# Attention stage of a hybrid mLSTM and attention layer: elementwise work moved from POOL to VectorE, a gate folded into a scaled eviction, and softmax denominators applied to the head's result

## The chip, the cores and the metric

One core of a Trainium2 chip runs the whole layer in one launch. The metric is the device time of that core in microseconds: the median of three runs before the change is 1370.47 us (1370.43 to 1371.47). Names used below: PE is TensorE, DVE is VectorE, ACT is ScalarE, POOL is GpSimd, and SP is SyncE, which issues the DMAs.

## The reference

The layer works on 512 tokens of width 1024 in float32. It runs a feed-forward block, a mixing block and a second feed-forward block, each as a modulated residual. The mixing block is what the change touches; cut to the parts that matter:

```python
z = u @ w_mix + b_mix                       # q, k, v of both branches, their gates
h_m = mlstm_chunkwise(q_m, k_m, v_m, i_m, f_m)            # 4 heads, 256 wide
y_a = jax.nn.sigmoid(o_m) * rms_norm(h_m, mlstm_norm_g)
# forgetting attention, 16 heads of 64
q, k = rms_norm(q, q_g), rms_norm(k, k_g)
F = jnp.cumsum(jax.nn.log_sigmoid(f_pre), axis=1)
logits = einsum(q_blk, k) * 64 ** -0.5 + (F_blk[..., :, None] - F[..., None, :])
p = softmax(where(causal, logits, -inf))
y_b = einsum(p, v)
merged = jax.nn.sigmoid(g_a) * (y_a @ w_branch_a) + jax.nn.sigmoid(g_b) * (y_b @ w_branch_b)
x = x + g2 * (merged @ w_out)
```

## The kernel before

Every float32 matrix product is made of three passes on PE with operands split into a high and a low part (mm3, L106 to L110: high x high, low x high, high x low). A weight arrives as a tile `raw` (L76 to L80, a DMA that SP issues, three buffers); `split` (L82 to L92) lets ACT copy its high part to `wh` (L89) and DVE subtract that to make `wl` (L91), four buffers each.

The program is written for a tile framework with a scheduler. It puts the instructions of each engine in an order of its own choice and places the semaphores; each engine then runs its list strictly in that order. A tile of a tag with n buffers waits until the n-th tile before it is no longer read.

The attention stage is the loop over n in 18 of `run` (L1024 to L1042), about 547 to 856 us of the span. PSUM serves it with four banks `g` for projections and four banks `t` for all else. For each of the 16 heads it takes these steps, staggered so that head n's scores, head n-1's transposes and head n-2's result are in flight together:

- `fox_s(n)`, L779 to L807: a DMA spreads the head's row of cumulative gates over the partitions (A0, L784); POOL adds the causal mask to it (Am, L787, 128x512). PE makes the scores of four query blocks in four t banks (L795, L796), DVE evicts them with bias and running minimum (L798, L802), and ACT takes the exponentials into S (L806), whose row sums become `sm`, one 128x4 tile.
- `fox_p(n-1)`, L809 to L838: DVE takes the reciprocal of sm (L813) and scales the four blocks of S by it (L816); PE transposes S (L824); ACT and DVE evict the result as high part Ph (L822) and low part Pl (L823).
- `fox_o(n-2)`, L840 to L858: eight matmuls with the split values fvt (L854) give the high and the low half of the values' product in two halves of a bank; ACT copies the one (yt, L857), DVE adds the other and writes 64 rows of yb (L858).
- `fox_t`, L749 to L777: for each pair of heads PE transposes the token tiles tk (L767), and ACT and DVE make the split q and k (fq, fk, klz; L772 to L776).

Between these steps the loop pulls pieces of projections (`fill`) that keep PE busy: `fox_qkv(g)` (L700 to L747) for groups of four heads, `gate` (L882 to L895) and, from head 12 on, `y_a` (L861 to L879). In `fox_qkv` the four token tiles tk hold q and k of four heads; after their mean squares, DVE makes the factors rq (L125 to L135) and POOL scales the four tiles (L728). The values are evicted with bias by DVE (vg, L733), and for each of four token blocks ACT writes the high parts of two pairs of heads (fvt, L736, two 128x128) and POOL the low parts (L737). In `y_a` ACT takes a tanh (L869), POOL turns it into 0.5 + 0.5 tanh (L870), and DVE multiplies it with the gain and the transposed mLSTM output from PSUM (ya, L877).

Of the kernel before, what the change touches and what calls it, by code (L numbers as in the profile page):

```python
# [11 lines left out]
F32 = mybir.dt.float32  # L12
F32R = mybir.dt.float32r
I32 = mybir.dt.int32
AF = mybir.ActivationFunctionType
# [5 lines left out]
P = 128  # L21
T = 512
NT = 4
D = 1024
NK = 8
# [21 lines left out]
class Layer:  # L47
# [568 lines left out]
    def v_mlstm(self, half, ap, ip):  # L616
        nc, w = self.nc, self.A["w_mix"][0]
        bb = self.bias_bcast([(VM + half * 512, 512)], ip)
        vt = []
        for i in range(2):  # L620
            pair = [ap.tile([P, NT, 258], F32R, name=self.nm("vm"), tag="vm", bufs=6) for _ in range(2)]
            nc.scalar.activation(pair[0][:, :, 256:258], self.onz, AF.Copy)
            nc.scalar.activation(pair[1][:, :, 256:258], self.onz, AF.Copy, scale=0.0)
            vt.append(pair)
        def done(tb, ps):
            f = self.tmp(ip, "vf")
            nc.vector.tensor_tensor(f, ps, bb, op=ADD)
            for i in range(2):
                hi, lo = vt[i]
                s = slice(i * 256, (i + 1) * 256)  # L630
                nc.scalar.activation(hi[:, tb, 0:256], f[:, s], AF.Copy)
                nc.vector.tensor_tensor(lo[:, tb, 0:256], f[:, s], hi[:, tb, 0:256], op=SUB)
        def mk(ch):
            def make():
                wh, wl = self.w_mov(w, ch * 256, VM + half * 512)
                return wh, wl, 2 * ch, 2
            return make
        self.vt[2 * half:2 * half + 2] = vt
        yield from self.u_gemm_tokens([mk(c) for c in range(4)], 512, done)
# [60 lines left out]
    def fox_qkv(self, g, ip):  # L700

        nc, sp, w = self.nc, self.sp, self.A["w_mix"][0]
        o = g * 256
        bb = self.bias_bcast([(QF + o, 256), (KF + o, 256)], ip)
        tok = [ip.tile([P, 512], F32, name=self.nm("tk"), tag="tok", bufs=4) for _ in range(NT)]
        ss = sp.tile([P, NT, 8], F32, name=self.nm("fs"), tag="fs", bufs=2)
        def done(tb, ps):
            nc.vector.tensor_tensor(tok[tb], ps, bb, op=ADD)  # L708
            j = self.tmp(ip, "fj")
            nc.scalar.activation(j, tok[tb], AF.Square)  # L710
            nc.vector.tensor_reduce(ss[:, tb, :], j.rearrange("p (h d) -> p h d", h=8), AX.X, ADD)
        def mk(ch):
            def make():
                sh = [P, 2, 512]
                rows = w[ch * 256:(ch + 1) * 256]
                r = self.raw(sh, [(lambda t, i=i: t[:, :, i * 256:(i + 1) * 256],
                                   rows[:, c + o:c + o + 256].rearrange("(k p) n -> p k n", p=P))
                                  for i, c in enumerate((QF, KF))])
                wh, wl = self.split(r, sh)
                return wh, wl, 2 * ch, 2  # L720
            return make
        yield from self.u_gemm_tokens([mk(c) for c in range(4)], 512, done)
        v = sp.tile([P, NT * 8], F32, name=self.nm("fv"), tag="fv", bufs=2)
        nc.vector.tensor_scalar(v, ss.rearrange("p b h -> p (b h)"), 1.0 / 64, EPS, op0=MUL, op1=ADD)
        r = self.rsqrt(v, NT * 8)
        for tb in range(NT):
            t3 = tok[tb].rearrange("p (h d) -> p h d", h=8)
            nc.gpsimd.tensor_tensor(t3, t3, r[:, tb * 8:(tb + 1) * 8].unsqueeze(2).to_broadcast([P, 8, 64]), op=MUL)  # L728
        bv = self.bias_bcast([(VF + o, 256)], ip)
        vt = [ip.tile([P, NT, 2, P], F32R, name=self.nm("fvt"), tag="vm", bufs=6) for _ in range(2)]  # L730
        def donev(tb, ps):
            f = ip.tile([P, 256], F32, name=self.nm("vg"), tag="t2", bufs=3)
            nc.vector.tensor_tensor(f, ps[:, :256], bv[:, :256], op=ADD)  # L733
            for pr in range(2):
                f2 = f[:, pr * P:(pr + 1) * P].rearrange("p (h d) -> p h d", h=2)
                nc.scalar.activation(vt[pr][:, tb, :, 0:64], f2, AF.Copy)  # L736
                nc.gpsimd.tensor_tensor(vt[pr][:, tb, :, 64:P], f2, vt[pr][:, tb, :, 0:64], op=SUB)  # L737
        def mkv(ch):
            def make():
                sh = [P, 4, 256]  # L740
                r = self.raw(sh, [(lambda t: t, w[ch * 512:(ch + 1) * 512, VF + o:VF + o + 256]
                                   .rearrange("(k p) n -> p k n", p=P))])
                wh, wl = self.split(r, sh)
                return wh, wl, 4 * ch, 4
            return make
        self.fx[g] = (tok, vt)
        yield from self.u_gemm_tokens([mkv(c) for c in range(2)], 256, donev)  # L747
# [31 lines left out]
    def fox_s(self, h, ip):  # L779
# [4 lines left out]
        nc.sync.dma_start(A0, self.A_d[h:h + 1, :].to_broadcast([P, T]))  # L784
        Am = ip.tile([P, T], F32, name=self.nm("Am"), tag="bc", bufs=4)
        b4 = lambda t: t.rearrange("p (b t) -> p b t", b=NT)
        nc.gpsimd.tensor_tensor(b4(Am), b4(A0), self.maskF[:, None, :].to_broadcast([P, NT, P]), op=ADD)  # L787
        S = ip.tile([P, 1280], F32, name=self.nm("S"), tag="p6", bufs=5)
        mn = sp.tile([P, NT, 2], F32, name=self.nm("mn"), tag="mn", bufs=4)
        sm = sp.tile([P, NT], F32, name=self.nm("sm"), tag="sm", bufs=4)  # L790
        for qb in range(NT):
# [12 lines left out]
                m = mn[:, qb, 1:2]  # L804
            ws = slice(o, o + (qb + 1) * P)
            nc.scalar.activation(S[:, ws], S[:, ws], AF.Exp, scale=-1.0, bias=m, accum_out=sm[:, qb:qb + 1])  # L806
        self.S[h] = (S, sm)  # L807

    def fox_p(self, h, ip):  # L809

        nc = self.nc
        S, sm = self.S[h]
        nc.vector.reciprocal(sm, sm)  # L813
        for qb in range(NT):
            ws = slice(P_OFF[qb], P_OFF[qb] + (qb + 1) * P)
            nc.vector.tensor_scalar(S[:, ws], S[:, ws], sm[:, qb:qb + 1], None, op0=MUL)  # L816
        Ph = ip.tile([P, 1408], F32R, name=self.nm("Ph"), tag="p6", bufs=5)
        Pl = ip.tile([P, 1408], F32R, name=self.nm("Pl"), tag="p6", bufs=5)
        nc.scalar.activation(Ph[:, 512:640], self.ident, AF.Copy, scale=0.0)
        nc.scalar.activation(Pl[:, 512:640], self.ident, AF.Copy, scale=0.0)  # L820
        def evac(b, n, o):
            nc.scalar.activation(Ph[:, o:o + n], b[:, :n], AF.Copy)  # L822
            nc.vector.tensor_tensor(Pl[:, o:o + n], b[:, :n], Ph[:, o:o + n], op=SUB)  # L823
        tr = lambda b, c, qb, kb: nc.tensor.transpose(b[:, c:c + P], S[:, P_OFF[qb] + kb * P:P_OFF[qb] + (kb + 1) * P], self.ident)  # L824
        b = self.tbank()
        for qb in range(NT):
            tr(b, qb * P, qb, 0)
        evac(b, 512, 0)
        b = self.tbank()
        tr(b, 0, 3, 3)  # L830
        for qb in range(1, NT):
            tr(b, qb * P, qb, 1)
        evac(b, 512, 640)
        b = self.tbank()
        for qb in range(2, NT):
            tr(b, (qb - 2) * P, qb, 2)
        evac(b, 256, 1152)
        self.S[h] = (Ph, Pl)  # L838

    def fox_o(self, h, ip):  # L840
# [10 lines left out]
        for kb, o, q0 in blk:  # L851
            for Px in (Ph, Pl):
                n += 1
                nc.tensor.matmul(po[:, q0:], vt[pr][:, kb, i % 2, :], Px[:, o:o + T - q0], start=n == 1, stop=n == 8)  # L854
        tmp = self.tmp(ip, "yt")
        ot = slice(64 - hb, 128 - hb)
        nc.scalar.activation(tmp[rows, :], po[ot, :], AF.Copy)  # L857
        nc.vector.tensor_tensor(self.yb[2 * g + pr][rows, :], po[rows, :], tmp[rows, :], op=ADD)  # L858


    def y_a(self, m, ap, ip):  # L861
# [5 lines left out]
        self.gemm_stat(ps, w, 0, T, range(4, 8))  # L867
        th = self.tmp(ip, "th")
        nc.scalar.activation(th, ps, AF.Tanh, scale=0.5, bias=self.hom[:, m:m + 1])  # L869
        nc.gpsimd.tensor_scalar(th, th, 0.5, 0.5, op0=MUL, op1=ADD)  # L870
        ht = ip.tile([P, NT, P], F32, name=self.nm("ht"), tag="tok", bufs=4)
        nc.sync.dma_start(ht, self.h_d[:, m * P:(m + 1) * P].rearrange("(b p) n -> p b n", p=P))
        b = self.tbank()
        for tb in range(NT):
            nc.tensor.transpose(b[:, tb * P:(tb + 1) * P], ht[:, tb, :], self.ident)
        ya = ap.tile([P, T], F32, name=self.nm("ya"), tag="qk", bufs=16)
        nc.vector.scalar_tensor_tensor(ya, b, self.colA[:, R_MG + m:R_MG + m + 1], th, op0=MUL, op1=MUL)  # L877
        self.ya[m] = ya
        yield  # L879

# [41 lines left out]
    def run(self):  # L922
        nc, tc, A = self.nc, self.tc, self.A
        gain = lambda r: self.colA[:, r:r + NK]
        self.x_d = self.dp.tile([T, D], F32, name="x_d")
        self.h_d = self.dp.tile([T, D], F32, name="h_d")
        self.g_d = [self.dp.tile([P, T], F32, name=f"g_d{i}") for i in range(2 * NK)]

        self.ntmp, self.xn_tiles = 5, self.xn_start
# [60 lines left out]
        with tc.tile_pool(name="att", bufs=1) as ip:  # L990
# [9 lines left out]
            nc.gpsimd.memset(self.onz[:, :, 1:2], 0.0)  # L1000
            self.hom = ip.tile([P, NK], F32, name="hom")
            nc.vector.tensor_scalar(self.hom, self.colA[:, R_OM:R_OM + NK], 0.5, None, op0=MUL)
            self.hgg = yp.tile([P, 2 * NK], F32, name="hgg")
            nc.vector.tensor_scalar(self.hgg, self.colA[:, R_GG:R_GG + 2 * NK], 0.5, None, op0=MUL)
            self.klz = [None] * 2
# [112 lines left out]
```

## Time and profile before

| | us |
|---|---|
| median of three runs | 1370.47 (1370.43 to 1371.47) |
| the profiled execution | 1369.97 |
| its span | 1367.9 |
| PE busy | 1345.7 |
| DVE busy | 795.1 |
| ACT busy | 557.0 |
| POOL busy | 115.5 |

The granted clock of TensorE is 0.999 of full speed throughout. A row of a group of instructions gives line, engine, operation, output and inputs (buffer numbers left out), shapes and count; after the first bar the busy time and the mean of one in ns; after the second the idle time of the engine just before them and what ended it. A row of the timeline gives start and length in us. A row of the waits gives who waited for what: us in total, times, longest. In the table by slices the columns are the stretch, its length, and the busy time of PE, of PE's weight loads, of DVE, ACT and POOL with their instruction counts.

### The profile page before, as it was taken

What the parts mean: (1) busy time and instruction counts of PE and PEld (TensorE: products, weight loads), DVE (VectorE), ACT (ScalarE), POOL (GpSimd) and SP (SyncE); (2) the same over time, 40 slices, a digit from 0 to 9 for tenths busy, and PEclk for the clock granted to TensorE, in tenths of its full rate; (3) what the DMA queues carried; (4) which work ended last, traced back from release to release, by engine and by line L of the source; (5) the groups of instructions that cost most, each with busy time, mean ns of one, the idle gap of its engine ahead of it and who ended that gap; (6) DMA issues with size and microseconds to landing.
All of it is one profiled execution on the core that took longest, in us unless ns stands there. A gap on an engine that the chain in (4) does not pass through costs nothing.

```text
span 1367.9 us, 17550 instructions
## 1 busy us (share of the span) xinstructions
PE 1345.7 (98%) x6586; PEld 1126.2 (82%) x6586; DVE 795.1 (58%) x1427; ACT 557.0 (41%) x953; POOL 115.5 (8%) x143
## 2 busy tenths in 40 slices
PE   7999999999999999999999999999999999999998
PEld 6788887877888888888888888888798888888886
DVE  6865666656467777785776775456473333332232
ACT  4542333323237655466655665332263223222120
POOL 2000000000011100321121311012010000000000
PEclk9999999999999999999999999999999999999999
DMA  9676556666534434434252542464323333333330
GB/s 289 189 216 194 182 182 191 216 214 192 184 79 110 124 94 129 144 90 137 57 155 62 162 108 70 131 192 145 94 78 108 94 105 95 92 100 101 100 123 31
DMA packets 216457, 183.37 MB, mean 134 GB/s; under 512 B 10866, under 2 KB 182546, under 8 KB 216372
## 3 DMA queue, kind: packets, MB, share of 16 engines
q1 hardware_dynamic: 215892, 182.17, 44.5%
q8 instruction: 52, 0.85, 0.3%
q14 instruction: 33, 0.27, 0.1%
q0 software_dynamic: 416, 0.06, 0.0%
q10 hardware_dynamic: 64, 0.02, 0.0%
HBM read 172.18 MB, written 10.03 MB: 133 GB/s over the span
## 4 chain that ended last, share of the span: by engine, by line
PE 90%; DVE 6%; ACT 3%; issue 1%; DMA 1%; SPq 0%; DVEq 0%; ACTq 0%
PE g L110 23%; PE g L108 23%; PE g L109 23%; PE t L108 4%; PE t L110 4%; PE t L109 4%; PE g L510 2%; PE t L854 2%; PE t L824 1%; DVE wl L91 1%; PE t L795 1%; PE t L796 1%; PE t L510 1%; DVE fq L774 0%; ACT uh L475 0%
## 5 line engine op out<-in xcount | busy, mean ns | idle before, releaser
L91 DVE TENSOR_TENSOR wl<-raw,wh 128x1024 fp32r<-128x1024 f32 x214 | 274.5, 1284 | 280.1 <-ACT wh L89 262.5
L89 ACT ACTIVATE wh<-raw 128x1024 fp32r<-128x1024 f32 x214 | 225.8, 1060 | 496.8 <-PE g L109 153.1
L108 PE MATMUL g<-uh,wh 128*128 128x512 f32 (+2 forms) x984 | 370.5, 377 | 0.5 <-ACT wh L89 0.5
L110 PE MATMUL g<-uh,wl 128*128 128x512 f32 (+2 forms) x984 | 369.7, 376 | 1.2 <-DVE wl L91 1.2
L109 PE MATMUL g<-ul,wh 128*128 128x512 f32 (+2 forms) x984 | 369.7, 376 | 0.0
L110 PEld LDWEIGHTS g<-uh,wl 128*128 128x128 f32 (+1 forms) x984 | 184.6, 188 | 35.9 <-DVE wl L91 2.0
L108 PEld LDWEIGHTS g<-uh,wh 128*128 128x128 f32 (+1 forms) x984 | 184.7, 188 | 34.4 <-ACT wh L89 1.2
L109 PEld LDWEIGHTS g<-ul,wh 128*128 128x128 f32 (+1 forms) x984 | 184.8, 188 | 33.2
L108 PE MATMUL g<-wh,uh 128*128 128x512 f32 (+1 forms) x320 | 111.9, 350 | 0.0
L110 PE MATMUL g<-wh,ul 128*128 128x512 f32 (+1 forms) x320 | 111.1, 347 | 0.0
L109 PE MATMUL g<-wl,uh 128*128 128x512 f32 (+1 forms) x320 | 111.0, 347 | 0.0
L325 DVE TENSOR_TENSOR sl<-g,sl 128x512 f32<-128x512 f32 (+1 forms) x45 | 29.9, 666 | 82.8 <-PE g L110 82.7
L284 DVE SCALAR_TENSOR_TENSOR acc<-raw,ccol,acc 128x1024 f32<-128x1024 f32 x49 | 62.8, 1281 | 14.4 <-DMA raw<-in_w_ada_dram 13.6
L108 PE MATMUL g<-wh,hh 128*128 128x512 f32 x176 | 69.2, 393 | 0.0
L110 PE MATMUL g<-wh,hl 128*128 128x512 f32 x176 | 69.1, 393 | 0.0
L108 PE MATMUL t<-wh,hh 128*128 128x512 f32 x176 | 69.0, 392 | 0.0
L109 PE MATMUL g<-wl,hh 128*128 128x512 f32 x176 | 69.0, 392 | 0.0
L109 PE MATMUL t<-wl,hh 128*128 128x512 f32 x176 | 69.0, 392 | 0.0
L110 PE MATMUL t<-wh,hl 128*128 128x512 f32 x176 | 69.0, 392 | 0.0
L108 PEld LDWEIGHTS g<-wh,uh 128*128 128x128 f32 x320 | 60.5, 189 | 7.9 <-DVE tk L708 0.5
L110 PEld LDWEIGHTS g<-wh,ul 128*128 128x128 f32 x320 | 60.5, 189 | 7.8
L109 PEld LDWEIGHTS g<-wl,uh 128*128 128x128 f32 x320 | 60.5, 189 | 7.4
(267 smaller groups left out, 1900.4 us busy)
## 6 DMA issues: line engine op xcount, KB each, us to landing
raw<-in_ffn_w_in_dram SPq DMA_DIRECT2D x82, 512.0 KB
raw<-in_w_ada_dram SPq DMA_DIRECT2D x56, 512.0 KB
raw<-in_w_mix_dram SPq DMA_DIRECT2D x48, 512.0 KB
raw<-in_ffn_w_out_dram SPq DMA_DIRECT2D x44, 512.0 KB
ar<-in_w_ada_dram SPq DMA_DIRECT2D x32, 256.0 KB
raw<-in_w_mix_dram SPq DMA_DIRECT2D x32, 256.0 KB
A<-A_d SPq DMA_DIRECT2D x16, 256.0 KB
raw<-in_w_branch_a_dram SPq DMA_DIRECT2D x8, 512.0 KB
```

The source lines that it names most:

```text
L89: nc.scalar.activation(hi, src, AF.Copy)
L91: nc.vector.tensor_tensor(lo, src, hi, op=SUB)
L108: mm(ps, lh, rh, start=start, stop=False)
L109: mm(ps, lh, rl, start=False, stop=False)
L110: self.last_mm = mm(ps, ll, rh, start=False, stop=stop)
L284: nc.vector.scalar_tensor_tensor(acc, r, self.ccol[:, k:k + 1], acc, op0=MUL, op1=ADD)
L325: nc.vector.tensor_tensor(s[:, :w], ps_b[:, c0:c1], s[:, :w], op=MUL)
L510: mm = nc.tensor.matmul(acc_ps[b], (wl if p == 1 else wh)[:, b % 2, s], self.ul[k] if p == 2 else self.uh[k], start=k == 0 and p == 0, sto ...
L795: nc.tensor.matmul(ps[:, :w], q[:, s], k[:, :w], start=True, stop=False)
L796: nc.tensor.matmul(ps[:, :w], q[:, s], kl[:, :w], start=False, stop=True)
L824: tr = lambda b, c, qb, kb: nc.tensor.transpose(b[:, c:c + P], S[:, P_OFF[qb] + kb * P:P_OFF[qb] + (kb + 1) * P], self.ident)
L854: nc.tensor.matmul(po[:, q0:], vt[pr][:, kb, i % 2, :], Px[:, o:o + T - q0], start=n == 1, stop=n == 8)
```

## The change

1. **tk** (L728, now L729): the four scalings of a group go from POOL to DVE.
2. **fvt**: the two tiles of a group, one for each pair of heads, become one tile of four heads. One ACT copy and one subtraction of 128x256 replace two and two of 128x128, and the subtraction goes from POOL to DVE. The mLSTM values that share the tag are paired the same way (six buffers become three of twice the size).
3. **Am** (L787): the add goes from POOL to DVE.
4. **Denominators**: S is no longer scaled (64 DVE instructions gone). The reciprocal moves into `fox_s`; SP writes its 128x4 to DRAM (r_d) and reads it back as rows, spread over the 64 partitions of yb that the head will fill (32 new DMAs). `fox_o` adds into yt and then multiplies by those rows (16 new DVE instructions).
5. **ya**: POOL's 0.5 + 0.5 tanh goes. ACT evicts the transposed output scaled by half the gain (hmg, made once), and DVE computes (tanh + 1) times that, from SBUF.

```diff
-            pair = [ap.tile([P, NT, 258], F32R, name=self.nm("vm"), tag="vm", bufs=6) for _ in range(2)]
+            t = ap.tile([P, 2, NT, 258], F32R, name=self.nm("vm"), tag="vm", bufs=3)
+            pair = t[:, 0], t[:, 1]
...
-            nc.gpsimd.tensor_tensor(t3, t3, r[:, tb * 8:(tb + 1) * 8].unsqueeze(2).to_broadcast([P, 8, 64]), op=MUL)
+            nc.vector.tensor_tensor(t3, t3, r[:, tb * 8:(tb + 1) * 8].unsqueeze(2).to_broadcast([P, 8, 64]), op=MUL)
...
-        vt = [ip.tile([P, NT, 2, P], F32R, name=self.nm("fvt"), tag="vm", bufs=6) for _ in range(2)]
+        vt = ip.tile([P, NT, 4, P], F32R, name=self.nm("fvt"), tag="vm", bufs=3)
...
-            for pr in range(2):
-                f2 = f[:, pr * P:(pr + 1) * P].rearrange("p (h d) -> p h d", h=2)
-                nc.scalar.activation(vt[pr][:, tb, :, 0:64], f2, AF.Copy)
-                nc.gpsimd.tensor_tensor(vt[pr][:, tb, :, 64:P], f2, vt[pr][:, tb, :, 0:64], op=SUB)
+            f4 = f.rearrange("p (h d) -> p h d", h=4)
+            nc.scalar.activation(vt[:, tb, :, 0:64], f4, AF.Copy)
+            nc.vector.tensor_tensor(vt[:, tb, :, 64:P], f4, vt[:, tb, :, 0:64], op=SUB)
...
-        nc.gpsimd.tensor_tensor(b4(Am), b4(A0), self.maskF[:, None, :].to_broadcast([P, NT, P]), op=ADD)
+        nc.vector.tensor_tensor(b4(Am), b4(A0), self.maskF[:, None, :].to_broadcast([P, NT, P]), op=ADD)
...
-        self.S[h] = (S, sm)
+
+        nc.vector.reciprocal(sm, sm)
+        nc.sync.dma_start(self.r_d[h].rearrange("b p -> p b"), sm)
+        rows = slice(h % 2 * 64, h % 2 * 64 + 64)
+        nc.sync.dma_start(self.yb[h // 2][rows, :].rearrange("p (b t) -> p b t", b=NT),
+                          self.r_d[h][None, :, :].to_broadcast([64, NT, P]))
+        self.S[h] = S
...
-        S, sm = self.S[h]
-        nc.vector.reciprocal(sm, sm)
-        for qb in range(NT):
-            ws = slice(P_OFF[qb], P_OFF[qb] + (qb + 1) * P)
-            nc.vector.tensor_scalar(S[:, ws], S[:, ws], sm[:, qb:qb + 1], None, op0=MUL)
+        S = self.S[h]
...
-        nc.vector.tensor_tensor(self.yb[2 * g + pr][rows, :], po[rows, :], tmp[rows, :], op=ADD)
+        nc.vector.tensor_tensor(tmp[rows, :], po[rows, :], tmp[rows, :], op=ADD)
+        y = self.yb[2 * g + pr][rows, :]
+        nc.vector.tensor_tensor(y, tmp[rows, :], y, op=MUL)
...
-        nc.gpsimd.tensor_scalar(th, th, 0.5, 0.5, op0=MUL, op1=ADD)
...
-        nc.vector.scalar_tensor_tensor(ya, b, self.colA[:, R_MG + m:R_MG + m + 1], th, op0=MUL, op1=MUL)
+        nc.scalar.activation(ya, b, AF.Copy, scale=self.hmg[:, m:m + 1])
+        nc.vector.scalar_tensor_tensor(ya, th, 1.0, ya, op0=ADD, op1=MUL)
```

The scheduler orders each engine anew. The order of PE keeps its 6360 rows, with a few transposes and projection matmuls exchanged. Three places show what moves elsewhere.

DVE at the end of the third projection group (heads 8 to 11; about 681 us in the trace before). Before, vg is the evicted values, rq the factors of tk, and wl the low part of the next two weights:

```order
L733 TENSOR_TENSOR vg_6222<-g_6082,bb_6076 128x256
L135 SCALAR_TENSOR_TENSOR rq_6059<-rt_6060,rq_6059 128x32
L733 TENSOR_TENSOR vg_6240<-g_6083,bb_6076 128x256
L91 TENSOR_TENSOR wl_6324<-raw_6321,wh_6323 128x1024
L91 TENSOR_TENSOR wl_6388<-raw_6385,wh_6387 128x1024
L858 TENSOR_TENSOR yb_3226<-t_6246,yt_6255 64x512
L813 RECIPROCAL sm_6144<-sm_6144 128x4
```

The same place after the change:

```order
L734 TENSOR_TENSOR vg_6197<-g_6073,bb_6069 128x256
L135 SCALAR_TENSOR_TENSOR rq_6052<-rt_6053,rq_6052 128x32
L734 TENSOR_TENSOR vg_6213<-g_6074,bb_6069 128x256
L729 TENSOR_TENSOR tk_5772<-tk_5772,rq_6052 128x512
L729 TENSOR_TENSOR tk_5773<-tk_5773,rq_6052 128x512
L729 TENSOR_TENSOR tk_5774<-tk_5774,rq_6052 128x512
L729 TENSOR_TENSOR tk_5775<-tk_5775,rq_6052 128x512
L808 RECIPROCAL sm_6136<-sm_6136 128x4
L737 TENSOR_TENSOR fvt_6071<-vg_6197,fvt_6071 128x4x64
L737 TENSOR_TENSOR fvt_6071<-vg_6213,fvt_6071 128x4x64
L734 TENSOR_TENSOR vg_6229<-g_6075,bb_6069 128x256
L91 TENSOR_TENSOR wl_6307<-raw_6304,wh_6306 128x1024
```

The four scalings, the reciprocal and two of the fvt subtractions now stand ahead of the first wl, and the second wl has moved behind the head's result and the Pl.

DVE near head 12's reciprocal (about 794 us before). Before, Pl is the low part of the transposed S:

```order
L813 RECIPROCAL sm_7321<-sm_7321 128x4
L816 TENSOR_SCALAR S_7319<-S_7319,sm_7321 128x128
L816 TENSOR_SCALAR S_7319<-S_7319,sm_7321 128x256
L816 TENSOR_SCALAR S_7319<-S_7319,sm_7321 128x384
L816 TENSOR_SCALAR S_7319<-S_7319,sm_7321 128x512
L877 SCALAR_TENSOR_TENSOR ya_7398<-t_7393,colA,th_7388 128x512
L91 TENSOR_TENSOR wl_7701<-raw_7698,wh_7700 128x1024
L823 TENSOR_TENSOR Pl_7406<-t_7409,Ph_7405 128x512
```

The same place after the change:

```order
L860 TENSOR_TENSOR yt_7345<-t_7336,yt_7345 64x512
L808 RECIPROCAL sm_7290<-sm_7290 128x4
L862 TENSOR_TENSOR yb_3245<-yt_7345,yb_3245 64x512
L787 TENSOR_TENSOR Am_7553<-A_1344_7551,maskF 128x512
L881 SCALAR_TENSOR_TENSOR ya_7370<-th_7361,ya_7370 128x512
L825 TENSOR_TENSOR Pl_7374<-t_7377,Ph_7373 128x512
L825 TENSOR_TENSOR Pl_7374<-t_7384,Ph_7373 128x512
L825 TENSOR_TENSOR Pl_7374<-t_7391,Ph_7373 128x256
L91 TENSOR_TENSOR wl_7667<-raw_7664,wh_7666 128x1024
```

The scalings are gone, a multiply and an Am have come, and the wl stands behind the Pl.

SP around the loads of the same third group (A is the gates' row of a head, bb a bias, raw a weight). Before:

```order
L784 DMA A_1082_6138<-A_d 128x512
L79 DMA raw_6259<-in_w_mix_dram 128x8x128
L79 DMA raw_6321<-in_w_mix_dram 128x8x128
L79 DMA raw_6385<-in_w_mix_dram 128x8x128
L784 DMA A_1114_6339<-A_d 128x512
L79 DMA raw_6483<-in_w_mix_dram 128x8x128
```

After:

```order
L784 DMA A_1075_6130<-A_d 128x512
L79 DMA raw_6247<-in_w_mix_dram 128x8x128
L809 DMA r_d_84<-sm_5742 128x4x1
L811 DMA yb_3242<-r_d_84 64x512
L79 DMA raw_6304<-in_w_mix_dram 128x8x128
L79 DMA raw_6371<-in_w_mix_dram 128x8x128
L784 DMA A_1107_6322<-A_d 128x512
L809 DMA r_d_85<-sm_5904 128x4x1
L811 DMA yb_3242<-r_d_85 64x512
L79 DMA raw_6465<-in_w_mix_dram 128x8x128
```

Each write of r_d and the read that waits for it stand between loads of weights.

More of the change, by code (lines that the diff above doesn't have):

```diff
@@ L853, in fox_o @@
                 n += 1
-                nc.tensor.matmul(po[:, q0:], vt[pr][:, kb, i % 2, :], Px[:, o:o + T - q0], start=n == 1, stop=n == 8)
+                nc.tensor.matmul(po[:, q0:], vt[:, kb, i, :], Px[:, o:o + T - q0], start=n == 1, stop=n == 8)
         tmp = self.tmp(ip, "yt")
@@ L926, in run @@
         self.h_d = self.dp.tile([T, D], F32, name="h_d")
+        self.r_d = [self.dp.tile([NT, P], F32, name=f"r_d{h}") for h in range(16)]
         self.g_d = [self.dp.tile([P, T], F32, name=f"g_d{i}") for i in range(2 * NK)]
@@ L1002, in run @@
             nc.vector.tensor_scalar(self.hom, self.colA[:, R_OM:R_OM + NK], 0.5, None, op0=MUL)
+            self.hmg = ip.tile([P, NK], F32, name="hmg")
+            nc.vector.tensor_scalar(self.hmg, self.colA[:, R_MG:R_MG + NK], 0.5, None, op0=MUL)
             self.hgg = yp.tile([P, 2 * NK], F32, name="hgg")
```

## The prediction

> **What bounds the kernel now.** I read the page first: the busy time of each engine, then the chain that ended last.
>
> ```profile
> PE 1345.7 (98%) x6586; PEld 1126.2 (82%) x6586; DVE 795.1 (58%) x1427; ACT 557.0 (41%) x953; POOL 115.5 (8%) x143
> PE 90%; DVE 6%; ACT 3%; issue 1%; DMA 1%; SPq 0%; DVEq 0%; ACTq 0%
> ```
>
> TensorE (PE) is busy 98% of the span and carries 90% of the chain. VectorE (DVE), 58% busy, and POOL, 8% busy, can only matter where PE waits for them. So the question is not how much work the change saves, but which PE wait it removes or makes. The next view is the waits of PE inside the attention stage (547 to 856 us), then the busy time by engine in slices of 34.2 us of that stage: the second slice and the sum of the nine.
>
> ```profile
> PE t L108 <- DVE hn L688: 1.0, 1, 1.0
> PE t L795 <- DVE Pl L823: 0.6, 1, 0.6
> PE t L824 <- ACT fk L776: 0.3, 1, 0.3
> PE t L824 <- DVE fq L774: 0.3, 1, 0.3
> PE t L795 <- DVE fq L774: 0.2, 1, 0.2
> 581.40:615.60 34.20, 34.05 (x215) 30.63 (x214) 30.23 (x77) 21.92 (x50) 10.20 (x13) 1.00 0.32 90
> sum 307.80, PE 305.05 PEld 263.62 DVE 222.03 ACT 181.83 POOL 70.09; mean PE 33.89 PEld 29.29 DVE 24.67 ACT 20.20 POOL 7.79
> ```
>
> In 309 us PE waits five times, 2.4 us in all, and never for POOL or a DMA. By the slices PE is idle 307.80 - 305.05 = 2.75 us. The change leaves PE's instructions as they are (6360 before and after), so about 2.4 to 2.75 us is the most that it can gain here. DVE is 222.03/307.80 = 72% busy, 88% in its fullest slice (30.23 of 34.20): there is room, though not everywhere.
>
> **The change part by part.** Durations are from the profiled execution, 1369.97 us (span 1367.9 and 2.1 around it). The median is 0.5 higher, 1370.47.
>
> *DVE work.* The groups of instructions, and then the lines by themselves (minimum, median, maximum in ns):
>
> ```profile
> L816 DVE TENSOR_SCALAR S<-S,sm 128x128 f32<-128x128 f32 (+1 forms) x64 | 27.3, 484 | 0.5
> L787 POOL TENSOR_TENSOR Am<-A,maskF 128x512 f32<-128x512 f32 x16 | 23.5, 1469 | 133.1 <-DMA A<-A_d 112.9 <-DVE rt L131 17.8 <-issue 2.4
> L728 POOL TENSOR_TENSOR tk<-tk,rq 128x512 f32<-128x512 f32 x16 | 23.4, 1492 | 23.8 <-DVE rd L130 23.2 <-DVE rq L135 0.6
> L737 POOL TENSOR_TENSOR fvt<-vg,fvt 128x128 fp32r<-128x128 f32 x32 | 14.9, 496 | 37.6 <-ACT fvt L736 37.6
> L918 DVE TENSOR_TENSOR yl<-yb,yh 128x512 fp32r<-128x512 f32 x8 | 5.1, 682 | 0.0
> L632 DVE TENSOR_TENSOR vm<-vf,vm 128x256 fp32r<-128x256 f32 x16 | 6.1, 416 | 0.0
> L858 DVE TENSOR_TENSOR yb<-t,yt x16: 673/688/695, 608.4 to 849.0; 64x512 f32<-64x512 f32 x16
> ```
>
> Gone: 64 scalings of S, 27.3 us. Added: a 128x512 add or multiply of two SBUF tiles costs 0.68 us on DVE (L918), so 16 Am and 16 tk are 32 x 0.68 = 21.8; 16 fvt of 128x256 at 0.416 (L632) are 6.7; 16 more yb multiplies at 0.69 (L858) are 11.0. Net 39.5 - 27.3 = +12.2 us on 222, so 76% busy. The tk operand is broadcast along its last dimension, which no DVE row shows: its bounds are 0.68 and POOL's own 1.49 (L728). I take 0.68, the DVE row of the same size, and keep 1.49 for a rival. As PE waited for none of this work, its price is nothing as long as DVE meets PE's dates.
>
> *ACT.* 32 fvt copies at 0.298 become 16 of twice the width, at most 0.596 each, so no more in sum; eight new ya evictions cost about as much as the tanh of that size:
>
> ```profile
> L736 ACT ACTIVATE fvt<-vg 128x128 fp32r<-128x128 f32 x32 | 7.7, 298 | 7.3 <-DVE vg L733 7.2
> L869 ACT ACTIVATE th<-g,hom 128x512 f32<-128x512 f32 x8 | 5.4, 676 | 0.1
> L89 ACT ACTIVATE wh<-raw 128x1024 fp32r<-128x1024 f32 x41 | 43.4, 1059 | 52.1 <-PE g L110 26.3 <-PE g L109 25.3 <-ACT S L806 0.6
> ```
>
> That is 8 x 0.68 = 5.4 us at most on 181.83 of 307.80: hidden in ACT's idle time, of which the stage's weight copies alone (L89, third row) have 52.1 us, waiting for PE to free a buffer. If that cover failed, the eight evictions would cost 5.4 us.
>
> *SP and the way of the denominators.* Sixteen writes of sm and sixteen broadcast reads join SP's queue, between the weight loads. SP holds everything behind a read until the write has landed. The nearest row is a write to DRAM and the read of it, mod_d:
>
> ```profile
> 110.22 0.25 SPq L298 DMA_DIRECT2D mod_d<-br  x1
> 111.44 0.33 SPq L316 DMA_DIRECT2D gb<-mod_d  x1
> L813 DVE RECIPROCAL sm<-sm x16: 158/178/179, 575.3 to 828.5; 128x4 f32<-128x4 f32 x16
> ```
>
> From issue to issue 1.22 us, so a head holds SP for about 1.2 + 0.3 us, and for as long as the reciprocal is late. No weight copy of the stage waited for its load (the L89 row above names PE and ACT alone), so that hold is absorbed: I take 0, with 16 x 1.2 = 19.5 us as the other end if every hold reached PE. The row itself is needed late: the last reciprocal starts at 828.5, and the last yb at 849.0, 20.5 us for two transfers.
>
> The Trainium skill, page "DMA: Bandwidth & Descriptors", section "Specifications", speaks against the write: below 512 bytes a DMA engine does a read-modify-write, and sm goes out as 512 elements of 4 bytes. No run here shows such a write yet. By that rule the 1.2 us are too short: an estimate with four times as long, 4.9 us, leaves the sum as it is, since 20.5 us are there, and raises the far end of SP's holds to 16 x 4.9 = 78 us.
>
> *POOL.* Its stage work was on the way of PE only by slowing DVE. The first place, DVE, POOL and then PE on the timeline:
>
> ```profile
> 550.52 0.17 DVE L131 TENSOR_SCALAR rt<-rd 128x4 f32<-128x4 f32 x1
> 550.72 0.89 DVE L132 TENSOR_TENSOR rt<-rt,rd 128x4 f32<-128x4 f32 x1
> 550.55 4.05 POOL L728 TENSOR_TENSOR tk<-tk,rq 128x512 f32<-128x512 f32 x4 [23.17 <-DVE rd L130]
> 558.60 0.42 DVE L733 TENSOR_TENSOR vg<-g,bb 128x256 f32<-128x256 f32 x1 [0.68 <-POOL fvt L737]
> 559.59 1.33 DVE L91 TENSOR_TENSOR wl<-raw,wh 128x1024 fp32r<-128x1024 f32 x1 [0.56 <-ACT wh L89]
> 562.99 0.36 PE L108 MATMUL t<-vm,Wh 128*128 128x258 f32 x1 [0.99 <-DVE hn L688]
> ```
>
> While POOL scales tk (4.05 us), DVE's 128x4 operations take 0.89 instead of 0.17 us. Afterwards the scalings cost DVE 4 x 0.68 = 2.7 us, 1.3 less, and the 0.68 us for POOL's fvt goes; the four fvt cost 4 x 0.42 = 1.7. So DVE itself is about level, and what counts is the split at 559.59, which waits for ACT: with four fvt copies instead of eight ACT can be earlier. Of the 0.99 us between nothing and all can go; I take **0.7**.
>
> The second place, near 798 us:
>
> ```profile
> 794.56 1.64 DVE L816 TENSOR_SCALAR S<-S,sm 128x128 f32<-128x128 f32 x4
> 796.78 1.66 DVE L91 TENSOR_TENSOR wl<-raw,wh 128x1024 fp32r<-128x1024 f32 x1
> 795.89 1.46 POOL L787 TENSOR_TENSOR Am<-A,maskF 128x512 f32<-128x512 f32 x1
> 798.36 1.27 DVE L823 TENSOR_TENSOR Pl<-t,Ph 128x512 fp32r<-128x512 f32 x2
> 799.09 0.38 PE L795 MATMUL t<-fk,fq 128*128 128x256 f32 x1 [0.58 <-DVE Pl L823]
> ```
>
> PE waits for the first Pl, which stood behind a wl that POOL's Am had slowed. In the new order of DVE the Pl stand before that wl, and the four S scalings ahead of them are gone, against one Am and one multiply: even if ACT's new eviction holds Ph back by its 0.68 us, Pl comes about 1 us earlier (1.64 + 1.66 - 0.68 - 0.69 = 1.9, less what Ph loses). The **0.6** goes. What is late next is PE itself. The three ping-pong waits between transposes and fq or fk (0.8 us) stay.
>
> Sum: -0.7 - 0.6 = -1.3 us: 1368.7 by the profiled execution, and 0.5 more, **1369.2**, as a median.
>
> **Where it can turn: the tight place.** In two of the three later projection groups (near 682 and 755 us) the tk scalings and two fvt now stand on DVE ahead of a weight's wl. DVE, POOL and PE of the first of them:
>
> ```profile
> 681.43 0.17 DVE L135 SCALAR_TENSOR_TENSOR rq<-rt,rq 128x32 f32<-128x32 f32 x1
> 681.86 3.99 DVE L91 TENSOR_TENSOR wl<-raw,wh 128x1024 fp32r<-128x1024 f32 x2
> 681.75 7.00 POOL L728 TENSOR_TENSOR tk<-tk,rq 128x512 f32<-128x512 f32 x4 [0.21 <-DVE rq L135]
> 689.53 0.39 PE L110 MATMUL g<-uh,wl 128*128 128x512 f32 x1
> ```
>
> Before, the first wl ended at about 683.9 (half of the two) and PE took it at 689.53, 5.7 us later. Now: rq ends at about 682.2 (a yb multiply more stands ahead of it); then two vg 0.8, four tk 2.7, the reciprocal 0.2, two fvt 0.8 and the wl 1.2 without POOL beside it, 5.7 in all. That ends at 687.9 by the durations, and some 0.4 earlier because neighbours overlap a little on DVE (0.17 us from 681.43, and the next at 681.52): 687.5. About **2.0 us** are left, so PE doesn't wait. The load that waits for this wl starts 3.6 us later:
>
> ```profile
> 683.93 5.34 SPq L79 DMA_DIRECT2D raw<-in_w_mix_dram  x6
> 689.04 1.06 ACT L89 ACTIVATE wh<-raw 128x1024 fp32r<-128x1024 f32 x1 [1.84 <-PE g L109]
> 711.86 0.39 PE L108 MATMUL g<-wh,uh 128*128 128x512 f32 x1
> ```
>
> Its copy came 5.1 us after the issue; with the same 5.1 it moves from 689.0 to about 692.6, and what stands behind it on ACT with it. That weight's first matmul in PE's order is the one at 711.86, so I take 0; a failed cover would cost up to those 3.6 us.
>
> **Rivals.**
>
> 1. *Slower: DVE misses the two dates.* It decides from 2.0 us more ahead of the wl, that is from 0.68 + 2.0/4 = 1.2 us for a tk scaling with its broadcast operand. At POOL's 1.49 the four take 6.0 instead of 2.7 and PE waits 1.3 us in each place: 1369.2 + 2.6 = 1371.8. At the 7.0 us that POOL took for four beside DVE, it waits 2.3 twice: 1373.8. For it: DVE had no idle time in that stretch (no wait is named in the rows at 681.43 and 681.86), and 2.0 us is a small reserve. Against it: every DVE row of that size stands near 0.68. Chance 0.17, of which 0.10 lie over 0.2%.
> 2. *Slower: SP's holds reach the weights.* 1.2 us for each head, up to 1369.2 + 19.5 = 1388.7. Against it stands the L89 row of the stage. Chance 0.04.
> 3. *All of PE's waits go*, as banks come free earlier throughout: 2.4 to 2.75 us, 1368.1 to 1367.7 as a median. Nothing in the change speeds the fq and fk of L774 and L776 but the lighter queue of DVE's scalings. Chance 0.12, of which 0.06 pass 0.2%, with what the five waits don't show.
> 4. *The change does nothing for PE*: ACT sets the first place, and Pl waits for Ph at the second. 1370.5. Chance 0.12.
>
> **How the numbers follow.** The forecast, 1369.2, has 0.55 (1368.4 to 1370.2). A measurement of this kernel can tell about 0.2%, 2.7 us, from no change: faster is below 1367.7, slower above 1373.2. The forecast, rival 4, half of rival 3 and 0.07 of rival 1 lie within: 0.55 + 0.12 + 0.06 + 0.07 = 0.80. Faster 0.06, slower 0.10 + 0.04 = 0.14. The range goes from rival 3's end, 1367.7, to the dear end of rival 1, 1373.8; beyond it lie rival 2, half of rival 3 and what of rival 1 costs more than its rows.
>
> **What would show it.** In the profile after: no PE wait for hn L689 and none for Pl L825 where they were; L729 near 0.68 us on DVE, in four groups; the 128x4 operations at 0.16 throughout; no PE wait for wl near 682 and 755; weight copies (L89) that still wait for PE alone; no ACT or PE wait that goes back to r_d or yb. The forecast is wrong if L729 takes over 1.2 us, if PE waits for wl in those two places, or if weight copies begin to wait for raw.

## The result and the profile after

The change makes the kernel slower: 1403.70 us (1400.13 to 1406.09, five runs) against 1370.47 (1370.01 to 1371.47), a ratio of 1.0242 with a 95% interval of 1.0231 to 1.0253. The prediction was 1369.2, and its range ended at 1373.8.

The page of the profiled execution (span 1401.9 us) begins so; the second row is the chain that ended last:

```profile
PE 1355.1 (97%) x6586; PEld 1134.7 (81%) x6586; DVE 793.3 (57%) x1428; ACT 560.2 (40%) x945; POOL 46.2 (3%) x71
PE 79%; DVE 8%; DMA 8%; ACT 3%; issue 1%; SPq 0%; DVEq 0%; ACTq 0%
```

PE has lost 11 points of the chain, and DMA has 8 where it had 1. The waits of PE in the attention stage (547 to 890 us), then of SP, DVE and ACT, the rows that name a DMA:

```profile
PE t L826 <- DVE yt L860: 6.7, 2, 4.6
PE t L795 <- DVE Pl L825: 6.6, 1, 6.6
PE g L108 <- DVE tk L709: 4.5, 2, 3.9
PE t L767 <- DVE yt L860: 4.0, 1, 4.0
PE t L826 <- DVE fq L774: 3.0, 1, 3.0
PE t L826 <- DVE mn L802: 1.0, 1, 1.0
PE t L826 <- DVE Pl L825: 0.4, 1, 0.4
PE t L108 <- DVE hn L689: 0.4, 1, 0.4
PE t L826 <- ACT fk L776: 0.3, 1, 0.3
PE t L795 <- DVE fq L774: 0.2, 1, 0.2
```

```profile
SPq L811 <- DMA r_d<-sm: 137.5, 16, 11.0
```

```profile
DVE Am L787 <- DMA A<-A_d: 47.4, 9, 10.9
```

```profile
ACT wh L89 <- DMA raw<-in_w_mix_dram: 21.9, 2, 12.1
```

PE waits 27.1 us where it waited 2.4. It waits for DVE, but DVE has nothing more to do than before (793.3 us busy against 795.1); DVE waits itself, nine times, for a head's row of gates. Twice ACT waits for a weight. And SP stands 137.5 us, 8.6 for each head, until the write of r_d is done.

One of the stalls shows the whole chain. SP's, DVE's and PE's timelines at 821 to 832 us:

```profile
821.47 0.38 SPq L784 DMA_DIRECT2D A<-A_d  x1
821.95 0.41 SPq L809 DMA_DIRECT2D r_d<-sm  x1
831.57 0.45 SPq L811 DMA_DIRECT2D yb<-r_d  x1
```

```profile
820.89 0.67 DVE L862 TENSOR_TENSOR yb<-yt,yb 64x512 f32<-64x512 f32 x1
829.61 0.69 DVE L787 TENSOR_TENSOR Am<-A,maskF 128x512 f32<-128x512 f32 x1 [8.05 <-DMA A<-A_d]
830.22 0.69 DVE L881 SCALAR_TENSOR_TENSOR ya<-th,ya 128x512 f32<-128x512 f32 x1
830.82 1.61 DVE L825 TENSOR_TENSOR Pl<-t,Ph 128x512 fp32r<-128x512 f32 x3
```

```profile
831.56 0.58 PE L795 MATMUL t<-fk,fq 128*128 128x256 f32 x1 [6.58 <-DVE Pl L825]
```

The row of gates is issued half a microsecond before the write of r_d, and yet it arrives only at 829.6, 8.1 us later. For the first half of that time the DMA engines are at work (193 to 360 GB/s from 822 to 826); from 826.6 to 829.0 they move nothing, though the row has not arrived. Over the sixteen heads the median from the issue of a row to its add is 6.6 us, where it was 4.2 before. DVE runs its list in order: behind the Am that needs the row stand ya and Pl, and PE needs the bank that Pl empties. The read of r_d starts 9.6 us after the write.

The waits are not the whole loss: 27.1 - 2.4 = 24.7 us, and the span grew by 34.0. The rest is in PE's busy time, 1355.1 - 1345.7 = 9.4 us for the same 6586 matmuls. Five stretches around the stall at 597 us show it (length, PE, weight loads, DVE, ACT, POOL, then granted clock, DMA share, GB/s):

```profile
594.00:597.20 3.20, 2.59 (x12) 1.69 (x10) 3.09 (x6) 1.50 (x4) 0.00 (x0) 1.00 0.59 143
597.20:600.20 3.00, 0.02 (x1) 0.05 (x1) 2.90 (x5) 2.95 (x7) 0.00 (x0) 1.00 0.00 0
600.20:601.50 1.30, 1.30 (x11) 1.30 (x12) 1.30 (x3) 1.27 (x2) 0.00 (x0) 0.98 0.00 0
601.50:604.80 3.30, 3.30 (x18) 3.30 (x17) 3.24 (x6) 3.04 (x6) 0.00 (x0) 0.50 0.00 0
604.80:608.00 3.20, 3.20 (x25) 3.11 (x25) 2.67 (x17) 1.62 (x5) 0.00 (x0) 0.99 0.40 72
```

After 3.0 us without matmuls, and 1.3 us after work began again, PE is granted half its clock for 3.3 us, which costs about 1.6 us on top of the wait. Five such stretches lie in the stage, beginning near 601, 717, 758, 803 and 830 us, each after a stall; PE's busy time times the clock that is missing, in slices of 5 us, adds up to about 9.4 us (an estimate), all of what PE's busy time grew by. The Trainium skill, page "TensorE: Matmul & The Clock Gate", part 1 on the clock gate, says that PE falls to half its rate after an idle window of about 3.4 us and comes back after as long a busy one. The trace agrees in the ratio (0.50) and in the 3.3 us; here 3.0 us without a matmul were enough, with another wait of 0.6 us shortly before them.

### The profile page after: what moved, and what is told of

Its sections match the earlier page's. It is cut to its first block, busy times and chain, and to the rows that moved or that the text cites. A ratio compares the mean times of both kernels' runs of the same rounds, so it can differ in the third digit from the quotient of the medians.

```text
span 1401.9 us, 17468 instructions
## 1 busy us (share of the span) xinstructions
PE 1355.1 (97%) x6586; PEld 1134.7 (81%) x6586; DVE 793.3 (57%) x1428; ACT 560.2 (40%) x945; POOL 46.2 (3%) x71
## 4 chain that ended last, share of the span: by engine, by line
PE 79%; DVE 8%; DMA 8%; ACT 3%; issue 1%; SPq 0%; DVEq 0%; ACTq 0%
PE g L108 21%; PE g L110 20%; PE g L109 20%; PE t L110 4%; PE t L108 4%; PE t L109 4%; DMA A<-A_d 3%; DMA r_d<-sm 2%; PE g L510 2%; DVE wl L91 1%; DMA g_d<-tg 1%; DMA raw<-in_w_mix_dram 1%; PE t L856 1%; PE t L826 1%; PE t L510 1%
## 5 line engine op out<-in xcount | busy, mean ns | idle before, releaser
L91 DVE TENSOR_TENSOR wl<-raw,wh 128x1024 fp32r<-128x1024 f32 x214 | 269.3, 1260 | 292.6 <-ACT wh L89 276.4
L110 PEld LDWEIGHTS g<-uh,wl 128*128 128x128 f32 (+1 forms) x984 | 185.7, 189 | 36.5 <-DVE wl L91 2.1
```

Of the source, the lines that this page charges most:

```text
L91: nc.vector.tensor_tensor(lo, src, hi, op=SUB)
L110: self.last_mm = mm(ps, ll, rh, start=False, stop=stop)
```

## The experiments

The theory at the start, **H**: SP is held by the write of r_d, and what stands behind it comes late. The rivals: **D**, DVE has too much to do; **C**, the write stops the DMA engines themselves, whoever issues it; and on why the write is slow: **S** (later **N**), many small elements, against **L**, any round trip through DRAM, and **B**, elements that share a block. Each ratio is to the kernel before as measured in the same round: 1370.53 us for the first four runs, 1371.52 for the next four, 1371.21 for the last two.

### Without the denominators

```diff
+        self.S[h] = (S, sm)
...
         nc.vector.reciprocal(sm, sm)
-        nc.sync.dma_start(self.r_d[h].rearrange("b p -> p b"), sm)
...
-        self.S[h] = S
...
+            nc.vector.tensor_scalar(S[:, ws], S[:, ws], sm[:, qb:qb + 1], None, op0=MUL)
...
-        nc.vector.tensor_tensor(y, tmp[rows, :], y, op=MUL)
```

The read of r_d goes too, the reciprocal stands ahead of the scalings again, and the add writes yb itself.

> The change without its denominators: S is scaled on DVE as before, no r_d and no new DMAs; tk, fvt, Am and the gate stay as changed. Theory H (SP is held about 9.6 us per head by the write of r_d, and the gates' rows and weights behind it come late): the 33 us go, 1368 to 1371 us, no PE wait over 1 us in the stage. Rival D (DVE has too much to do in the tight places since it took POOL's work): DVE is even fuller here, 39 us more work than POOL's share left it, so the time stays above 1385.

1367.18 us, ratio 0.9978 (0.9969 to 0.9988). All of the loss is gone, and the four other parts of the change are a gain of 3.3 us. PE's waits in the stage, and the engines' busy time:

```profile
PE t L824 <- DVE fq L774: 0.5, 2, 0.3
PE t L108 <- DVE hn L689: 0.4, 1, 0.4
PE t L824 <- ACT fk L776: 0.3, 1, 0.3
PE t L795 <- DVE fq L774: 0.2, 1, 0.2
```

```profile
PE 1344.1 (98%) x6586; PEld 1126.5 (83%) x6586; DVE 802.0 (59%) x1476; ACT 561.1 (41%) x945; POOL 46.2 (3%) x71
```

DVE is busier here (802.0 us) than in the whole change (793.3), and PE waits 1.4 us: D falls. The work that came from POOL (16 Am, 16 tk, 16 fvt) measures 10.9 + 10.2 + 6.4 = 27.5 us on DVE, yet DVE's busy time rose by only 6.9. Some 16 of the other 20 us are what POOL had cost DVE by slowing it: the scalings of S fall from 27.3 to 20.7 us, the wl from 274.5 to 269.3, the factors of tk (rt and rq, L132 to L135) from 13.3 to 9.2. The rest isn't traced; neighbours that overlap on DVE count once in its busy time.

### The denominators alone

Before, with only the denominators' part of the change; POOL keeps tk, fvt, Am and the gate.

> The kernel before with the denominators alone changed (r_d, the multiplies); POOL keeps tk, fvt, Am and the gate. Theory H: SP is held as long, 16 times 9 to 10 us; the gates' rows come late for POOL's Am, and through it for the scores, and weights come late: slower than before by 5 to 33 us, less than the whole change only if DVE's waiting inside its list is a needed part. Rival D: DVE has less to do than before, so within 3 us of 1370.

1379.04 us, ratio 1.0065 (1.0047 to 1.0082): within the range of H, outside that of D. Alone the denominators' part costs 8.5 us; with the other four parts in place it costs 36.5 (1403.7 - 1367.2). POOL waits for the rows here. Behind such a wait stands the gate's tanh in POOL's list, behind that DVE's ya, and one long delay reaches PE that way:

```profile
POOL Am L787 <- DMA A<-A_d: 122.6, 10, 20.7
```

```profile
DVE ya L881 <- POOL th L874: 12.7, 8, 8.9
```

```profile
PE t L826 <- DVE ya L881: 6.5, 1, 6.5
```

### The write issued by POOL's queue

```diff
-        nc.sync.dma_start(self.r_d[h].rearrange("b p -> p b"), sm)
+        nc.gpsimd.dma_start(self.r_d[h].rearrange("b p -> p b"), sm)
```

The read of it likewise.

> The whole change, but POOL's queue issues the write of r_d and its read; the order of PE, DVE and ACT is that of the change. Theory H: SP is never held, 1368 to 1371 us, though write and read take as long. Rival D: stays near 1404. Rival C (the packets of 4 bytes crowd the DMA engines, whoever issues them): stays above 1385, with late weights.

1389.25 us, ratio 1.0135 (1.0119 to 1.0152). H alone is not enough, and C holds: SP is never held, but rows of gates and weights still come late, as DVE's and ACT's waits show:

```profile
DVE Am L787 <- DMA A<-A_d: 34.1, 10, 10.4
ACT wh L89 <- DMA raw<-in_w_mix_dram: 22.3, 3, 11.2
```

POOL's queue shows the same interval of 10 us, SP goes on issuing loads, and the stretches around it (the last two columns are DMA share and GB/s) show what becomes of them:

```profile
692.37 0.79 POOL L809 DMA_DIRECT2D r_d<-sm  x1 [17.41 <-DVE sm L808]
702.45 0.53 POOL L811 DMA_DIRECT2D yb<-r_d  x1 [9.29 <-DMA r_d<-sm]
```

```profile
694.25 0.89 SPq L79 DMA_DIRECT2D raw<-in_w_mix_dram  x2
```

```profile
692.40:695.90 3.50, 3.50 (x22) 3.01 (x21) 3.03 (x6) 2.38 (x5) 0.76 (x1) 1.00 1.55 43
695.90:702.90 7.00, 7.00 (x35) 5.91 (x34) 6.83 (x21) 0.69 (x1) 0.45 (x1) 1.00 0.56 7
702.90:706.40 3.50, 3.50 (x17) 2.90 (x16) 0.00 (x0) 0.00 (x0) 0.08 (x1) 1.00 0.84 224
```

With half a megabyte of weights issued at 694.25, the DMA engines move 7 GB/s for seven microseconds and 224 GB/s once the write is done. The weights' packets of 1024 bytes that do go through between 699.5 and 701.5 us take 2.6 to 3.0 us each; the median in the stage is 0.05.

### The write in runs of 16 bytes

```diff
-        nc.sync.dma_start(self.r_d[h].rearrange("b p -> p b"), sm)
+        nc.sync.dma_start(self.r_d[h].rearrange("b (p c) -> (b p) c", c=NT), sm)
```

> The whole change, but the write of r_d keeps sm's own order: 128 runs of 16 bytes instead of 512 elements of 4 (the denominators then land at permuted tokens; work and order of all engines are those of the change). Theory S (the hold comes from the 512 small elements): the time from write to read falls from 9.6 us to about a quarter, 2 to 3.5 us, and the kernel to 1369 to 1376. Rival L (any write to DRAM and back takes this long behind the weight loads): stays at 9 to 10 us and near 1404.

1367.00 us, ratio 0.9974 (0.9963 to 0.9985), with the order of PE, DVE and ACT unchanged. One head's write and read on SP, and SP's waits for the write in the stage:

```profile
657.67 0.34 SPq L809 DMA_DIRECT2D r_d<-sm  x1
660.06 0.45 SPq L811 DMA_DIRECT2D yb<-r_d  x1
```

```profile
SPq L811 <- DMA r_d<-sm: 24.5, 13, 4.0
```

From 9.6 to 2.4 us (over the sixteen heads the median from the issue of the write to that of the read goes from 10.1 to 2.7), and 24.5 us of waiting instead of 137.5. L falls: a round trip through DRAM is short, as mod_d's had been. The same two kilobytes cost 36.7 us of kernel time or nothing that can be measured (the change without its denominators takes 1367.18), by how they are cut.

### 128 elements of 4 bytes

```diff
-        nc.sync.dma_start(self.r_d[h].rearrange("b p -> p b"), sm)
+        nc.sync.dma_start(self.r_d[h][0:1, :].rearrange("b p -> p b"), sm[:, 0:1])
```

The read takes that row for all four blocks.

> The whole change, but only the first query block's 128 denominators are written, as 128 elements of 4 bytes into one row, and that row is spread over all four blocks (three blocks get wrong denominators; the order of all engines is that of the change). Theory N (the hold goes by the number of small elements): write to read falls to 3 to 4 us and the kernel to 1367 to 1372. Rival B (elements that share a block of 512 bytes wait for each other, and the four rows go side by side): stays at 8 to 10 us and near 1404.

1397.47 us, ratio 1.0183 (1.0169 to 1.0197). A quarter of the elements, and four fifths of the loss (29.3 of 36.5 us, each against the kernel before of its round): N falls. The median from write to read is 8.9 us. The time isn't spent in sending: the 128 packets leave between 652.8 and 654.0 us, some 9 ns each, and from then on the engines move 3 GB/s until the read is issued.

```profile
652.84 0.32 SPq L809 DMA_DIRECT2D r_d<-sm  x1
660.39 0.58 SPq L811 DMA_DIRECT2D yb<-r_d  x1
```

```profile
SPq L811 <- DMA r_d<-sm: 115.3, 16, 9.4
```

### 512 elements of 4 bytes, 512 bytes apart

```diff
-        nc.sync.dma_start(self.r_d[h].rearrange("b p -> p b"), sm)
+        nc.sync.dma_start(self.r_d[h][:, 0:1].rearrange("(b p) o -> p b o", p=P), sm[:, :, None])
```

A head's r_d has 512 rows here, each element goes to the start of one, and the first four rows are read.

> The whole change, but the 512 elements of 4 bytes go 512 bytes apart, each into a block of its own (the rows that are read back are filled once before, so the denominators that land are not the head's; the order of PE, DVE and ACT is that of the change). Rival B: the hold falls to 2 to 3 us and the kernel to 1367 to 1372. Theory N: it stays at 9 to 10 us, near 1404, and the other transfers stand still behind it as before.

1368.33 us, ratio 0.9976 (0.9967 to 0.9985).

```profile
659.84 0.37 SPq L809 DMA_DIRECT2D r_d<-sm  x1
661.84 0.45 SPq L811 DMA_DIRECT2D yb<-r_d  x1
```

```profile
SPq L811 <- DMA r_d<-sm: 21.6, 11, 3.9
```

As many elements of the same size, read from sm in the same pieces, but each written into a block of its own, and the write takes 2.0 us (median of the heads 2.6): B holds. What is slow is not the small element but 128 of them that fall into one 512-byte row of r_d; four such rows are written side by side in hardly more time than one (10.1 us against 8.9). The 16-byte write puts 32 runs into each row and is short, so a few may share one. How far apart is enough (512 bytes or less), and from how many on it hurts, was not tried.

### SP held, the DMA engines free

```diff
-        nc.sync.dma_start(self.r_d[h].rearrange("b p -> p b"), sm)
+        for _ in range(4):
+            nc.sync.dma_start(self.r_d[h].rearrange("b (p c) -> (b p) c", c=NT), sm)
```

> The whole change with the write as 128 runs of 16 bytes, made four times in a row into the same place, each after the one before (denominators permuted as in the 16-byte run). SP is held about 4 times 2 us, as long as in the change, but the DMA engines are free. If the hold of SP is the larger part of the loss: 1385 to 1400. If the standing still of the DMA engines is the larger part (the run with POOL's queue kept 19 of 33 us): 1368 to 1380.

1374.64 us, ratio 1.0024 (1.0014 to 1.0033). SP waits 95.0 us between the four writes and 33.5 before the reads, 128.5 in all, nearly as long as in the change (137.5), but in shorter pieces, and now and then a load goes out between two writes:

```profile
SPq L810 <- DMA r_d<-sm: 95.0, 39, 5.1
SPq L812 <- DMA r_d<-sm: 33.5, 16, 3.4
```

Against the single 16-byte write (1367.0) the hold costs about 7 us by itself: 7.6 by the two medians, 6.7 with each taken against the kernel before of its round. Against the same base the standing still of the engines, without a hold, costs 22.3 (1389.25), and both together 36.7. A hold of 9 us in one piece may cost more than these shorter ones: letting SP go in the change itself, in the run with POOL's queue, saved 14.5 (1403.70 - 1389.25). By either figure the hold is the smaller part.

### The denominators repaired

```diff
-        nc.sync.dma_start(self.r_d[h].rearrange("b p -> p b"), sm)
+        nc.sync.dma_start(self.r_d[h].rearrange("b (p c) -> (b p) c", c=NT), sm)
...
-        nc.vector.tensor_tensor(y, tmp[rows, :], y, op=MUL)
+        t4 = tmp[rows, :].rearrange("p (b t) -> p b t", b=NT)
+        nc.vector.tensor_tensor(t4, t4, y.rearrange("p (t b) -> p b t", b=NT), op=MUL)
+        nc.gpsimd.tensor_copy(y, tmp[rows, :])
```

> The whole change repaired: the write as 128 runs of 16 bytes, the rows read back in that order, and the multiply reads them with a stride of four elements; POOL copies the product to its place (16 copies). If the small elements are the whole loss: 1366.5 to 1368.5, level with the change without its denominators (1367.2). If the strided multiply or POOL's copies matter: 1369 or more.

1368.28 us, ratio 0.9979 (0.9970 to 0.9988). It beats the kernel before by 3.2 us, and it is level with the change without its denominators (3.3 us, ratio 0.9978): the 64 scalings that they save were never waited for.

### Am back on POOL

```diff
-        nc.vector.tensor_tensor(b4(Am), b4(A0), self.maskF[:, None, :].to_broadcast([P, NT, P]), op=ADD)
+        nc.gpsimd.tensor_tensor(b4(Am), b4(A0), self.maskF[:, None, :].to_broadcast([P, NT, P]), op=ADD)
```

> The whole change, but POOL makes Am as before; the denominators' write stays as changed (512 elements of 4 bytes into four rows, from SP). If the late rows of the gates cost so much because DVE waits for them inside its list, with wl, evictions and yb behind: POOL takes the wait and the kernel falls to 1375 to 1390, with DVE's waits for wl to ACT left. If the late weights and yb rows are the larger part: it stays at 1395 to 1405.

1383.34 us, ratio 1.0096 (1.0075 to 1.0117). With the slow write in place, 20 of the 36.5 us are there because the add stands in DVE's list (which is otherwise that of the change but for a few places). POOL waits four times as long for the rows as DVE did, mostly because it has nothing else to do: in this stage its list holds the sixteen adds alone, and nothing else waits in it:

```profile
POOL Am L787 <- DMA A<-A_d: 197.8, 12, 22.9
```

### The rows of gates from POOL's queue

```diff
-        nc.sync.dma_start(A0, self.A_d[h:h + 1, :].to_broadcast([P, T]))
+        nc.gpsimd.dma_start(A0, self.A_d[h:h + 1, :].to_broadcast([P, T]))
```

> The whole change, but POOL's queue issues the gates' rows (A0), so that SP's hold doesn't delay their issue; the write stays as changed. If the hold in front of A0 is the larger part: 1370 to 1382. If the standing still of the DMA engines is (A0 then arrives late though it was issued early): 1385 to 1400.

1396.57 us, ratio 1.0177 (1.0152 to 1.0201), 7 us less than the change. Issued past SP's hold, the rows still arrive late, as they must if the engines that carry them stand still:

```profile
DVE Am L787 <- DMA A<-A_d: 39.0, 10, 13.2
```

## Why the prediction was wrong

**The step that failed** is the one on SP and the way of the denominators. It took 1.2 us for the write, from the write and read of mod_d, and priced the hold at nothing; the write of sm takes 9.6 us, and with the rest of the change it costs 36.5. mod_d's row is of another kind: it is one contiguous row of 4 KB, its 1.2 us is what a round trip costs, and the 16-byte runs (2.4) and the elements 512 bytes apart (2.0) are near it. The write of sm is long because 128 elements share each row of r_d. The row of mod_d was the nearest in its path and far in its shape.

**The cover was the wrong one.** The step argued from the weight copies, which never waited for a load, and from the 20.5 us until a head's row is used. Both have that reserve, and with a short write it does cover them. But a hold and a standstill delay every transfer, and the rows of gates had no such reserve: the Am row quoted in the prediction names 112.9 us of POOL waiting for A0, and without any write DVE waits 12.8 us for them (the Am row below). On POOL the wait was harmless: tk, fvt and the gate stood behind it in POOL's list, but no wait of PE led back to them. The change moves the add, and with it the wait, into DVE's list, and the prediction priced the 0.68 us of the add and not its wait. The run with Am on POOL puts 20 us on this.

**Rival 2 had the cause and neither the price nor the way.** It held SP 1.2 us a head, asked whether weights come late, and ended at 1388.7 with a chance of 0.04. The estimate beside the Trainium skill's rule, four times as long, was nearer, though the factor was a guess, and it was judged by the same wrong cover. The rival also left out that the write stops the DMA engines for others: that, not SP's hold, is the larger part (22.3 us by itself against about 7).

**The Trainium skill's rule** (page "DMA: Bandwidth & Descriptors", section "Specifications": below 512 bytes a read-modify-write) pointed at the right place. As a price it doesn't separate the runs: 16-byte runs and single elements far apart lie below 512 bytes too and are fast. That elements which share a block wait for each other's read-modify-write would fit the four shapes that were measured; the runs show the dependence on place, and that the time passes after the packets have left, not the mechanism inside the DMA engine or the memory.

**The clock** was not in the prediction at all: about 9.4 us lost at half clock after waits.

**What held.** The durations were right; the Am and fvt rows of the change without its denominators, and the tk line of the whole change:

```profile
L787 DVE TENSOR_TENSOR Am<-A,maskF 128x512 f32<-128x512 f32 x16 | 10.9, 684 | 12.8 <-DMA A<-A_d 12.8
L737 DVE TENSOR_TENSOR fvt<-vg,fvt 128x256 fp32r<-128x256 f32 x16 | 6.4, 417 | 0.2 <-ACT fvt L736 0.2
```

```profile
L729 DVE TENSOR_TENSOR tk<-tk,rq x16: 683/686/693, 550.8 to 778.5; 128x512 f32<-128x512 f32 x16
```

They measure 0.68, 0.42 and 0.69 us against 0.68, 0.42 and 0.68, so rival 1, a dear tk scaling, is out. In no run does PE wait for a wl in the stage, so the two tight places hold. Without the slow write, the first place keeps 0.4 of its 0.99 us (forecast 0.3) and the wait for Pl is gone, as forecast. DVE's net work was forecast as +12.2 us and measured -1.8, partly because POOL's slowing of DVE (9 us on wl, rt and rq, by their rows) had been counted only at two places. Had the write cost what mod_d's does, the forecast would have been about 2 us too high: 1369.2 against the 1367.0 of the 16-byte runs. That is also 0.7 us past the 2.75 that the prediction called the most to be gained: in the change without its denominators PE's waits of the stage fall by only 1.0 us (2.4 to 1.4), and its busy time falls by 1.6 (1345.7 to 1344.1), for a reason that no run shows. Of the signs that the prediction named, weight copies that wait for raw did show (21.9 us); with the 16-byte write they wait 6.0 us as well, and PE loses nothing by it.

## What to carry to other kernels

A transfer is priced by its shape in the memory it writes: before a small tile is scattered to DRAM, count how many of its elements fall into one row, and write them as runs or apart. A wait that is free on an idle engine is not free on a busy one, so where an operation moves, move its row's idle column with it and look at what stands behind it. And a reserve argued for one kind of transfer (weights) says nothing of another (a row that is fetched just in time).

## What the runs showed of the hardware

- A write of 128 elements of 4 bytes into one 512-byte row of DRAM took 8.9 us (7.4 to 11.8) to the issue of its dependent read, 512 of them into four rows 10.1 (8.3 to 14.4); 512 into rows of their own 2.6 (1.8 to 4.4), and 128 runs of 16 bytes 2.7 (1.4 to 5.9): medians and extremes of sixteen heads each.
- While such a write is under way, the core's DMA engines carry almost nothing else: 7 GB/s over seven microseconds with weights queued, 224 GB/s right after, when POOL's queue issued the write; nothing from 826.6 to 829.0 us, when SP's did. A transfer issued 0.5 us before such a write was held up as well (it arrived after 8.1 us).
- A stall of PE can be paid twice: 3.0 us without a matmul were followed by 3.3 us at half clock, while a wait of 2.1 us (at 636.7) was not.
